# A dense transformer block on one core: the first four products of the MLP placed ahead of the last transposes of the second chunk

## The chip, the cores and the metric

The kernel runs on one core of a Trainium2 chip. The metric is the device time of one execution in microseconds (us), as the median of several runs.

## The reference

One block works on 2048 tokens of width 1024 in fp32. An input projection feeds attention and a pooling mixer; both are merged by gates, go through an output projection, and then

```python
x = _layernorm(ALPHA * x + g1 * y, ln1_g[l], ln1_b[l])
x = _mlp_sublayer(x, sh2, sc2, g2, w_mlp_in[l], w_mlp_out[l], ln2_g[l], ln2_b[l])

def _mlp_sublayer(z, shift, scale, gate, w1, w2, g, b):
    u = _modulate(z, shift, scale)            # _layernorm(z) * (1 + scale) + shift
    h = jnp.square(jax.nn.relu(u @ w1)) @ w2  # w1 1024 x 4096, w2 4096 x 1024
    return _layernorm(ALPHA * z + gate * h, g, b)
```

The change lies where the normalised tokens become the operand of `u @ w1`.

## The kernel before

**Stages.** Attention comes first, over all tokens. Then the merge, the output projection and the first normalisation run over two chunks of 1024 tokens, `c` = 0 and 1. Then comes the MLP's first product for both chunks, and then its second.

**The end of a chunk.** `out_mm` accumulates the output projection of one block of 128 tokens (`b`, 8 in a chunk); `ln_affine` normalises it, SP stores it as x1 (L956), and `ln1_u` normalises it again into a tile `xn` (`normal`, L900 on ACT). `u2_half(h)` turns four such blocks into the MLP's operand: for each of four pairs of 128 columns (`kp`), PE transposes eight 128x128 tiles (L929), ACT scales and shifts the two results into `u2f` (L930), and POOL forms four sums and differences `u2s` of quarters (L935 to L938). SP stores the three quarters that go as they are (L941) and the four combinations (L942). These are the seven *planes* of the scratch `us_scr[c]`. Half 0 runs inside the block loop; half 1 is put into the list `late`. Chunk 0's is run within chunk 1; chunk 1's is run behind the loop by `run(late)`, ahead of the MLP.

**The MLP's first product** multiplies 2x2 block matrices with seven products in place of eight. `us_scr[c]` holds the seven left operands, one plane each. The right operands are made from the weights of one `Pair` (256 columns of w1): `Pair.load` brings them into `sraw` (L1001, two DMAs of half a megabyte), `Pair.add` makes their combinations on POOL (`ext`, L1009 to L1011). fp32 is computed as three products of two rounded parts: `split` casts to the high part on ACT (L59) and subtracts it on DVE for the low part (L62). `Pair.step` splits a right operand into a tile `R` (8 buffers); `l_fill` loads a plane into `rw` (L1085, one DMA of a megabyte, 2 buffers) and splits it in two halves into `La` or `Lb`; all seven planes of a chunk stay for its 16 pairs. `Pair.prod` is one product: 12 matmuls of 128x512 (4 slices times 3 terms, L1039), and behind it a copy, a sum or a square in tiles `st`.

```python
ORDER = (1, 6, 2, 7, 5, 4, 3)
PLANE = {1: 0, 2: 1, 4: 2, 5: 3, 6: 4, 7: 5, 3: 6}
groups = [pairs[0:2]] + [[q] for q in pairs[2:14]] + [pairs[14:16], pairs[16:18]] + [[q] for q in pairs[18:]]
seq = [(g, p, q) for g in groups for p in ORDER for q in g]
```

So pairs 0 and 1 go together: the first four products of `seq` are product 1 of both and product 6 of both, 48 matmuls on planes 1 and 6; product 2 is next. Right operands are prepared `AHEAD` = 7 products ahead.

**What sets the order.** Each engine works through its own instructions in order, and so does SP, whose queue issues all DMAs here. PE's order is the order in which the code is written (`manual_schedule`); the other engines' is set by a scheduler when the kernel is built. Memory comes from pools that open and close like a stack on one side of SBUF: `lpx`, `ptx` and `rpx` hold the tiles of the chunk (with the `xn`, `u2f` and `u2s` slots) and close before `mlp` (`R`, `La`) and `mlp1` (`sraw`, `rw`, `Lb`, `st`, `ext`) open.

Of the kernel before, what the change touches and what calls it, by code (L numbers as in the profile page):

```python
# [16 lines left out]
P = 128  # L17
# [19 lines left out]
def block_kernel(  # L37
# [687 lines left out]
    for c in range(2):  # L725
# [195 lines left out]
        def u2_half(h, c=c, t0=t0, xn=xn, ys=ys):  # L921

            for kp in range(4):
# [38 lines left out]
        late = [lambda f=u2_half: f(1)]  # L962

    sp.dma_start(g2_scr, gb[1][0:1, :].rearrange("a d -> (a d)"))
    run(late)
    lpx.close()
# [11 lines left out]
    mp = ctx.enter_context(sbuf("mlp"))  # L978
    m1 = ExitStack()
    m1p = m1.enter_context(sbuf("mlp1"))  # L980
# [3 lines left out]
    def rtile():  # L984
        return mp.tile([P, 2, 4, P], F32R, name="R", tag="R", bufs=8)

    def sttile(name):
        return m1p.tile([P, 512], F32, name=name, tag="st", bufs=14)
# [3 lines left out]
    class Pair:  # L992
# [5 lines left out]
        def load(self):  # L998
            self.raw = m1p.tile([P, 2, 4, 256], F32, name="sraw", tag="sraw", bufs=3)
            for k in range(2):  # L1000
                sp.dma_start(self.raw[:, k], w1v[:, k, :, self.n * 256:(self.n + 1) * 256])  # L1001
            b11, b12, b21, b22 = self.b = [self.raw[:, k, :, h * P:(h + 1) * P] for k in range(2) for h in range(2)]
            self.op = {1: b11, 2: b21, 3: b22, 4: b11, 7: b12}

        def add(self):
            b11, b12, b21, b22 = self.b
            for p in (5, 6):
                self.op[p] = m1p.tile([P, 4, P], F32, name="ext", tag="ext", bufs=4)
            pool.tensor_tensor(self.op[5], b12, b11, ALU.subtract)  # L1009
            pool.tensor_tensor(self.op[6], b22, self.op[5], ALU.subtract)  # L1010
            pool.tensor_tensor(b12, b22, b12, ALU.subtract)  # L1011
# [70 lines left out]
    def l_fill(c, p):  # L1082

        raw = m1p.tile([P, 4, 512], F32, name="rw", tag="rw", bufs=2)
        sp.dma_start(raw, us_scr[c][:, PLANE[p]])  # L1085
        Lc[c][p] = []
        for j in range(2):
            if (p, j) in ((1, 0), (1, 1), (6, 0)):
                t = m1p.tile([P, 2, 2, 512], F32R, name="Lb", tag="Lb", bufs=3)
            else:  # L1090
                t = mp.tile([P, 2, 2, 512], F32R, name="La", tag="La", bufs=11)
            split(t[:, 0], t[:, 1], raw[:, 2 * j:2 * j + 2])
# [8 lines left out]
    AHEAD = 7  # L1101
    for i in range(AHEAD):
        if i % 2 == 0:
            l_fill(0, ORDER[i // 2])
        prep[i][1].step(prep[i][0])
    for p in ORDER[4:]:
        l_fill(0, p)
    for i, (g, p, q) in enumerate(seq):
        n = q.c * 16 + q.n
        if p == 1 and n + 2 < len(pairs):  # L1110
# [18 lines left out]
    def w2_fill(p, j):  # L1129
# [24 lines left out]
        l = mp.tile([P, 2, 2, 512], F32R, name="La", tag="La", bufs=11)  # L1154
# [3 lines left out]
    L2 = {p: [] for p in ORDER}  # L1158
    R2 = {}
# [160 lines left out]
```

## Time and profile before

| what | value |
|---|---|
| median of 3 runs | 3034.75 us (3033.85 to 3036.7) |
| profiled execution | 3039.96 us, its span 3038.2 us |
| granted clock of TensorE, mean over the span | 0.979 |
| PE busy | 2909.0 us, 96% of the span |
| DVE, ACT, POOL busy | 1819.1, 1369.1, 1380.6 us |
| matmuls of the first MLP product on `La`, on `Lb` | 485.2 us (2112), 139.5 us (576) |
| idle of PE just before the 576 on `Lb` | 25.4 us |

The profiled execution is one of its own, 5.2 us above the median of the others; all moments below are on its clock, in us from the start of the span. The last row of the table is almost all of the idle time that lies between the output projection of the second chunk and the MLP, where the change is made.

### The profile page before, as it was taken

How to read it: one execution, taken by the hardware profiler on the slowest of the kernel's cores; microseconds unless marked ns; L12 is line 12 of the kernel's file. 1: busy time of each engine (PE TensorE's matmuls, PEld its weight loads, DVE VectorE, ACT ScalarE, POOL GpSimd, SP SyncE). 2: the span in 40 equal slices, each digit the busy share in tenths (PEclk: the TensorE clock that was granted, in tenths of full speed). 3: DMA queues.
4: the chain of work that ended last, by engine and by line, in shares of the span. 5: the costliest groups of instructions: out<-in, count | busy, mean ns of one | idle time of the engine just before them, and what ended most of it. 6: DMA issues, size and time to landing. Idle time of an engine off the chain costs nothing. (4 is left out here: it accounts for less than half of the span.)

```text
span 3038.2 us, 42601 instructions
## 1 busy us (share of the span) xinstructions
PE 2909.0 (96%) x15336; PEld 2481.3 (82%) x15336; DVE 1819.1 (60%) x3201; ACT 1369.1 (45%) x2462; POOL 1380.6 (45%) x1638
## 2 busy tenths in 40 slices
PE   8899999999899999899999779999999799999998
PEld 5789989998888888888889668888888587888886
DVE  5577877877875444742144775557555453556675
ACT  3477767777741131432121455556555332333342
POOL 1867777777540014423032556657665240123244
PEclk9999999999999999999999889999999899999999
DMA  7111111112234433342122475547554684566563
GB/s 255 35 32 37 32 37 31 38 42 61 67 100 144 127 125 111 112 144 78 56 97 84 141 263 161 153 149 222 156 153 124 246 308 153 187 215 218 196 209 108
DMA packets 343015, 395.38 MB, mean 130 GB/s; under 512 B 16785, under 2 KB 277009, under 8 KB 341010
## 3 DMA queue, kind: packets, MB, share of 16 engines
q1 hardware_dynamic: 342802, 392.64, 40.5%
q8 instruction: 121, 1.98, 0.3%
q14 instruction: 92, 0.75, 0.1%
HBM read 275.13 MB, written 117.44 MB: 129 GB/s over the span
## 5 line engine op out<-in xcount | busy, mean ns | idle before, releaser
L1220 PE MATMUL ps_y<-La,R 128*128 128x512 f32 x2688 | 619.4, 393 | 25.8 <-ACT R L59 12.1
L1220 PEld LDWEIGHTS ps_y<-La,R 128*128 128x128 f32 x2688 | 508.9, 190 | 136.4 <-ACT La L59 13.7
L1039 PE MATMUL ps_h<-La,R 128*128 128x512 f32 x2112 | 485.2, 390 | 0.3 <-ACT cx L1044 0.3
L1039 PEld LDWEIGHTS ps_h<-La,R 128*128 128x128 f32 x2112 | 397.2, 188 | 83.3 <-ACT cx L1044 0.7
L62 DVE TENSOR_TENSOR R<-hraw,R 128x512 fp32r<-128x512 f32 x224 | 198.0, 890 | 150.7 <-ACT R L59 150.2
L59 ACT CAST R<-hraw 128x512 fp32r<-128x512 f32 x224 | 137.6, 621 | 281.3 <-PE ps_y L1220 272.9
L62 DVE TENSOR_TENSOR pl<-ps_pt,ph 128x512 fp32r<-128x512 f32 x312 | 212.5, 686 | 70.5 <-ACT ph L59 68.6
L465 POOL TENSOR_SCALAR s<-s,sm 128x640 f32<-128x640 f32 (+1 forms) x256 | 201.6, 795 | 103.0 <-DVE sm L464 53.9
L462 ACT ACTIVATE s<-s,sm 128x641 f32<-128x641 f32 (+1 forms) x256 | 209.8, 820 | 70.2 <-DVE sm L456 69.8
L456 DVE CUSTOM_DVE_ANT_0 s<-ps_s,mask,nsink 128x640 f32<-128x640 f32 (+1 forms) x256 | 211.5, 863 | 29.8 <-PE ps_s L451 29.7
L59 ACT CAST ph<-ps_pt 128x512 fp32r<-128x512 f32 x312 | 179.3, 580 | 109.3 <-PE ps_pt L486 106.0
L861 POOL TENSOR_TENSOR sa<-sa,m 128x512 f32<-128x512 f32 x32 | 57.1, 1805 | 374.5 <-DVE sa L860 374.5
L486 PE MATMUL ps_pt<-ident,s 128*128 128x128 f32 x1248 | 189.7, 274 | 12.4 <-DVE pl L62 8.2
L62 DVE TENSOR_TENSOR R<-sraw,R 128x512 fp32r<-128x512 f32 x160 | 146.3, 917 | 77.3 <-ACT R L59 76.8
L59 ACT CAST wh<-raw 128x2048 fp32r<-128x2048 f32 (+1 forms) x38 | 67.0, 1771 | 276.1 <-DMA raw<-w_in 73.6
L486 PEld LDWEIGHTS ps_pt<-ident,s 128*128 128x128 f32 x1248 | 151.6, 141 | 43.1 <-DVE pl L62 11.3
L62 DVE TENSOR_TENSOR wl<-raw,wh 128x2048 fp32r<-128x2048 f32 (+1 forms) x38 | 86.3, 2274 | 159.5 <-ACT wh L59 159.5
L59 ACT CAST R<-sraw 128x512 fp32r<-128x512 f32 x160 | 98.9, 621 | 155.2 <-PE ps_h L1039 97.5
L1039 PE MATMUL ps_h<-Lb,R 128*128 128x512 f32 x576 | 139.5, 396 | 25.4 <-ACT Lb L59 21.9
L1039 PEld LDWEIGHTS ps_h<-Lb,R 128*128 128x128 f32 x576 | 109.8, 191 | 49.7 <-ACT Lb L59 22.3
L66 PE MATMUL ps_out<-wh,mg 128*128 128x256 f32 x512 | 143.1, 281 | 0.0
L67 PE MATMUL ps_out<-wl,mg 128*128 128x256 f32 x512 | 142.8, 280 | 0.0
(264 smaller groups left out, 7098.4 us busy)
## 6 DMA issues: line engine op xcount, KB each, us to landing
hraw<-hs_scr SPq DMA_DIRECT2D x112, 512.0 KB, 4.0
w<-w_mlp_out SPq DMA_DIRECT2D x72, 512.0 KB, 5.4
sraw<-w_mlp_in SPq DMA_DIRECT2D x64, 512.0 KB, 6.3
hs_scr<-s SPq DMA_DIRECT2D x96, 256.0 KB, 4.6
raw<-w_in SPq DMA_DIRECT2D x19, 1024.0 KB, 5.5
raw<-w_ada SPq DMA_DIRECT2D x16, 1024.0 KB, 5.3
rw<-us_scr SPq DMA_DIRECT2D x14, 1024.0 KB, 5.4
raw<-u_scr SPq DMA_DIRECT2D x8, 1032.0 KB, 5.5
```

The costliest lines, as they stand in the source:

```text
L59: act.copy(hi, src)
L62: (lo_eng or dve).tensor_tensor(lo, src, hi.bitcast(F32), ALU.subtract)
L66: pe.matmul(ps, sh, mh, start=first, stop=False)
L67: pe.matmul(ps, sh, ml, start=False, stop=False)
L456: dve.tensor_tensor_reduce(out=s[:, 0:n], in0=pieces[z][2], in1=mk[z], op0=ALU.add, op1=ALU.min, scale=-1.0 / math.sqrt(HD), scalar=nsink[ ...
L462: act.activation(s[:, 0:n + 1], s[:, 0:n + 1], AF.Exp, bias=sm[:, 0, j:j + 1], scale=-1.0, accum_out=sm[:, 1, j:j + 1])
L465: pool.tensor_scalar(s[:, 0:n], s[:, 0:n], sm[:, 2, j:j + 1], 1.0, ALU.mult, ALU.mult)
L486: pe.transpose(pt[:, c:c + P], self.s.probs[2 * z + j][:, o:o + P], ident)
L861: pool.tensor_tensor(s, s, m0[j][:, a:a + m], ALU.add)
L1039: pe.matmul(ps, a, b, start=p in (1, 6, 5) and k == 0 and i == 0, stop=k == 3 and i == 2, skip_group_check=p not in (1, 6, 5))
L1220: pe.matmul(ps, a, b, start=n == 0 and z == 0, stop=n == 15 and z == 2)
```

## The change

`rpx` is still closed behind the chunk loop, but `lpx` stays open on the left side. Two pools, `mlpr` and `mlpr1`, are opened on the right side instead. They hold what the first four products need: all 8 buffers of `R`, four tiles `Le` for the halves of planes 1 and 6, 4 of the 14 `st` buffers (`se`), 2 of the 3 `sraw` buffers. Planes 1 and 6 are loaded as four half planes (L1099, half a megabyte each) into slots of `xs`, in place of two whole ones, and the first two pairs' `ext` lies in `xs` slots too. Chunk 1's half 1 of `u2_half` is cut in four pieces, one for each `kp`, whose `u2f` and `u2s` go to slots of `xs`. After product 4 of `seq` (`EARLY` = 4) these pieces run; then `lpx` is closed, `mlp` and `mlp1` are opened with the remaining buffers (`La` 7, `Lb` 3, `st` 10, `sraw` 1, `rw` 2, `ext` 4), planes 2, 7, 5, 4, 3 are filled (L1094) and pairs 2 and 3 are loaded. In the MLP's second product the left tiles are spread over the two sides in the same way (4 `Le` and 7 `La` for 11). Each engine executes as many instructions as before, SP two DMAs more.

```diff
--- before.py
+++ after.py
@@ -918,9 +918,9 @@
             normal(n, accs[b])
             xn.append(n)
 
-        def u2_half(h, c=c, t0=t0, xn=xn, ys=ys):
-
-            for kp in range(4):
+        def u2_half(h, kps=range(4), c=c, t0=t0, xn=xn, ys=ys):
+
+            for kp in kps:
                 f = slot(ys, 0, [P, 2, 512], F32, "u2f")
                 for kk in range(2):
                     k = 2 * kp + kk
@@ -959,11 +959,9 @@
             if b == 5:
                 u2_half(0)
         ln1_u(7)
-        late = [lambda f=u2_half: f(1)]
+        late = [lambda f=u2_half: f(1)] if c == 0 else [lambda kp=kp, f=u2_half, s=xs: f(1, (kp,), ys=s) for kp in range(4)]
 
     sp.dma_start(g2_scr, gb[1][0:1, :].rearrange("a d -> (a d)"))
-    run(late)
-    lpx.close()
     ptx.close()
     rpx.close()
 
@@ -975,17 +973,23 @@
 
     ORDER = (1, 6, 2, 7, 5, 4, 3)
     PLANE = {1: 0, 2: 1, 4: 2, 5: 3, 6: 4, 7: 5, 3: 6}
-    mp = ctx.enter_context(sbuf("mlp"))
+    ep = ctx.enter_context(sbuf("mlpr", side="right"))
     m1 = ExitStack()
-    m1p = m1.enter_context(sbuf("mlp1"))
+    e1 = m1.enter_context(sbuf("mlpr1", side="right"))
     ms3 = ExitStack()
     ms3.enter_context(tc.manual_schedule(engines={mybir.EngineType.PE}))
 
     def rtile():
-        return mp.tile([P, 2, 4, P], F32R, name="R", tag="R", bufs=8)
+        return ep.tile([P, 2, 4, P], F32R, name="R", tag="R", bufs=8)
+
+    m1p = None
+    sts = [0]
 
     def sttile(name):
-        return m1p.tile([P, 512], F32, name=name, tag="st", bufs=14)
+
+        n = sts[0] = (sts[0] + 1) % 14
+        pl, tag, bufs = (e1, "se", 4) if 1 <= n <= 4 else (m1p, "st", 10)
+        return pl.tile([P, 512], F32, name=name, tag=tag, bufs=bufs)
 
     w1v = w_mlp_in.rearrange("(k two p) n -> p two k n", two=2, p=P)
 
@@ -996,7 +1000,8 @@
             self.c, self.n, self.R = c, n, {}
 
         def load(self):
-            self.raw = m1p.tile([P, 2, 4, 256], F32, name="sraw", tag="sraw", bufs=3)
+            pl, bufs = (e1, 2) if (16 * self.c + self.n) % 3 < 2 else (m1p, 1)
+            self.raw = pl.tile([P, 2, 4, 256], F32, name="sraw", tag="sraw", bufs=bufs)
             for k in range(2):
                 sp.dma_start(self.raw[:, k], w1v[:, k, :, self.n * 256:(self.n + 1) * 256])
             b11, b12, b21, b22 = self.b = [self.raw[:, k, :, h * P:(h + 1) * P] for k in range(2) for h in range(2)]
@@ -1004,7 +1009,10 @@
 
         def add(self):
             b11, b12, b21, b22 = self.b
-            for p in (5, 6):
+            if m1p is None:
+                t = slot(xs, 1, [P, 2, 4, P], F32, "ext")
+                self.op.update({5: t[:, 0], 6: t[:, 1]})
+            for p in (5, 6) if m1p else ():
                 self.op[p] = m1p.tile([P, 4, P], F32, name="ext", tag="ext", bufs=4)
             pool.tensor_tensor(self.op[5], b12, b11, ALU.subtract)
             pool.tensor_tensor(self.op[6], b22, self.op[5], ALU.subtract)
@@ -1081,15 +1089,23 @@
 
     def l_fill(c, p):
 
-        raw = m1p.tile([P, 4, 512], F32, name="rw", tag="rw", bufs=2)
-        sp.dma_start(raw, us_scr[c][:, PLANE[p]])
+        if m1p is not None:
+            raw = m1p.tile([P, 4, 512], F32, name="rw", tag="rw", bufs=2)
+            sp.dma_start(raw, us_scr[c][:, PLANE[p]])
         Lc[c][p] = []
         for j in range(2):
-            if (p, j) in ((1, 0), (1, 1), (6, 0)):
+            if m1p is None:
+                half = slot(xs, 0, [P, 2, 512], F32, "rw")
+                sp.dma_start(half, us_scr[c][:, PLANE[p], 2 * j:2 * j + 2])
+            else:
+                half = raw[:, 2 * j:2 * j + 2]
+            if p in (1, 6):
+                t = ep.tile([P, 2, 2, 512], F32R, name="Le", tag="Le", bufs=4)
+            elif (p, j) in ((4, 1), (3, 0), (3, 1)):
                 t = m1p.tile([P, 2, 2, 512], F32R, name="Lb", tag="Lb", bufs=3)
             else:
-                t = mp.tile([P, 2, 2, 512], F32R, name="La", tag="La", bufs=11)
-            split(t[:, 0], t[:, 1], raw[:, 2 * j:2 * j + 2])
+                t = mp.tile([P, 2, 2, 512], F32R, name="La", tag="La", bufs=7)
+            split(t[:, 0], t[:, 1], half)
             Lc[c][p].append(t)
 
     pairs = [Pair(c, n) for c in range(2) for n in range(16)]
@@ -1099,15 +1115,23 @@
         q.load()
     prep = [(p, q) for _, p, q in seq]
     AHEAD = 7
+    EARLY = 4
     for i in range(AHEAD):
-        if i % 2 == 0:
+        if i in (0, 2):
             l_fill(0, ORDER[i // 2])
         prep[i][1].step(prep[i][0])
-    for p in ORDER[4:]:
-        l_fill(0, p)
     for i, (g, p, q) in enumerate(seq):
         n = q.c * 16 + q.n
-        if p == 1 and n + 2 < len(pairs):
+        if i == EARLY:
+            run(late)
+            lpx.close()
+            mp = ctx.enter_context(sbuf("mlp"))
+            m1p = m1.enter_context(sbuf("mlp1"))
+            for z in ORDER[2:]:
+                l_fill(0, z)
+            for z in (2, 3):
+                pairs[z].load()
+        if i >= EARLY and n + 2 >= 4 and p == 1 and n + 2 < len(pairs):
             pairs[n + 2].load()
         q.prod(p, Lc[q.c][p])
         if q is pairs[15]:
@@ -1151,11 +1175,14 @@
             pool.tensor_tensor(t, t, t2, ALU.subtract)
         else:
             t = b(1, 1)
-        l = mp.tile([P, 2, 2, 512], F32R, name="La", tag="La", bufs=11)
+        n = lns[0] = (lns[0] + 1) % 11
+        pl, tag, bufs = (ep, "Le", 4) if 1 <= n <= 4 else (mp, "La", 7)
+        l = pl.tile([P, 2, 2, 512], F32R, name="La", tag=tag, bufs=bufs)
         split(l[:, 0], l[:, 1], t)
         L2[p].append(l)
 
     L2 = {p: [] for p in ORDER}
+    lns = [0]
     R2 = {}
 
     def h_fill(p, i):
```

PE, from the transposes of half 1 of chunk 1 to the first products. Before (`ps_u` are the transposes, `ps_h` the products; a row is one run of equal instructions):

```order
L929 MATMUL ps_u_18090<-ident,xn 128x128 x4
L929 MATMUL ps_u_18106<-ident,xn 128x128 x4
L929 MATMUL ps_u_18112<-ident,xn 128x128 x4
L1039 MATMUL ps_h_18236<-Lb,R 128x512 x12
L1039 MATMUL ps_h_18257<-Lb,R 128x512 x12
L1039 MATMUL ps_h_18275<-Lb,R 128x512 x6
```

The same place after, from the third of the four products on:

```order
L1047 MATMUL ps_h_18142<-Le,R 128x512 x12
L1047 MATMUL ps_h_18160<-Le,R 128x512 x12
L929 MATMUL ps_u_18179<-ident,xn 128x128 x4
L929 MATMUL ps_u_18185<-ident,xn 128x128 x4
L929 MATMUL ps_u_18201<-ident,xn 128x128 x4
L929 MATMUL ps_u_18207<-ident,xn 128x128 x4
L929 MATMUL ps_u_18223<-ident,xn 128x128 x4
L929 MATMUL ps_u_18229<-ident,xn 128x128 x4
L929 MATMUL ps_u_18245<-ident,xn 128x128 x4
L929 MATMUL ps_u_18251<-ident,xn 128x128 x4
L1047 MATMUL ps_h_18106<-La,R 128x512 x12
```

The 48 matmuls of the first four products now stand ahead of the transposes of half 1, and product 2, on `La`, directly behind the last of these.

SP, the last stores of chunk 1 (`us_scr_62`) and the first loads of the MLP (weights, and planes from chunk 0's `us_scr_61`). Before:

```order
L942 DMA us_scr_62<-u2s 128x4x256
L941 DMA us_scr_62<-u2f 128x2x128 x6
L942 DMA us_scr_62<-u2s 128x4x256
L941 DMA us_scr_62<-u2f 128x2x128 x6
L942 DMA us_scr_62<-u2s 128x4x256 x3
L1001 DMA sraw<-w_mlp_in 128x4x256 x4
L1085 DMA rw<-us_scr_61 128x2048 x2
L1001 DMA sraw<-w_mlp_in 128x4x256 x2
L1085 DMA rw<-us_scr_61 128x2048 x5
```

The same place after:

```order
L942 DMA us_scr_62<-u2s 128x4x256
L1006 DMA sraw<-w_mlp_in 128x4x256 x4
L941 DMA us_scr_62<-u2f 128x2x128 x9
L942 DMA us_scr_62<-u2s 128x4x256
L941 DMA us_scr_62<-u2f 128x2x128 x3
L942 DMA us_scr_62<-u2s 128x4x256 x3
L1094 DMA rw<-us_scr_61 128x2048 x2
L1006 DMA sraw<-w_mlp_in 128x4x256 x2
L1094 DMA rw<-us_scr_61 128x2048 x2
```

The weights of the first two pairs now go ahead of the stores of half 1, planes 2 and 7 directly behind them.

SP earlier, among the stores of x1 of chunk 1 (`x_scr`), as a piece of the difference:

```order
 L667 DMA raw<-w_out 128x8x256
-L956 DMA x_scr<-acc 128x1024 x5
+L956 DMA x_scr<-acc 128x1024 x2
+L1099 DMA rw<-us_scr_61 128x1024 x2
+L956 DMA x_scr<-acc 128x1024
+L1099 DMA rw<-us_scr_61 128x1024
+L956 DMA x_scr<-acc 128x1024
+L1099 DMA rw<-us_scr_61 128x1024
+L956 DMA x_scr<-acc 128x1024
 L941 DMA us_scr_62<-u2f 128x2x128 x3
```

The four half planes of the first four products are loaded there.

## Rows read from the trace of the kernel before

**Rows 1.** The page's first part: busy us, share of the span, instructions.

```profile
PE 2909.0 (96%) x15336; PEld 2481.3 (82%) x15336; DVE 1819.1 (60%) x3201; ACT 1369.1 (45%) x2462; POOL 1380.6 (45%) x1638
```

**Rows 2.** PE's timeline: start, length, line, operation, count, idle before and releaser.

```profile
1711.25 1.04 PE L929 MATMUL ps_u<-ident,xn 128*128 128x128 f32 x8
...
1734.94 5.94 PE L929 MATMUL ps_u<-ident,xn 128*128 128x128 f32 x24 [0.66 <-ACT u2f L930]
1762.78 0.79 PE L1039 MATMUL ps_h<-Lb,R 128*128 128x512 f32 x1 [21.89 <-ACT Lb L59]
1764.07 7.77 PE L1039 MATMUL ps_h<-Lb,R 128*128 128x512 f32 x24 [0.50 <-DVE Lb L62]
1774.81 2.09 PE L1039 MATMUL ps_h<-Lb,R 128*128 128x512 f32 x5 [2.97 <-DVE Lb L62]
...
1780.41 28.73 PE L1039 MATMUL ps_h<-La,R 128*128 128x512 f32 x126
```

**Rows 3.** Windows: length, busy PE, PEld, DVE, ACT, POOL, clock, DMA share, GB/s.

```profile
1767.00:1768.00 1.00, 1.00 (x4) 0.79 (x3) 1.00 (x2) 1.00 (x2) 1.00 (x2) 0.50 0.91 139
...
1769.00:1770.00 1.00, 1.00 (x6) 0.84 (x5) 1.00 (x2) 1.00 (x2) 0.92 (x2) 1.00 0.97 410
...
1774.00:1775.00 1.00, 0.19 (x1) 0.20 (x2) 1.00 (x2) 0.42 (x1) 0.00 (x0) 1.00 0.00 0
...
1776.00:1777.00 1.00, 1.00 (x4) 0.81 (x3) 1.00 (x2) 0.00 (x0) 0.00 (x0) 0.50 0.40 66
...
1779.00:1780.00 1.00, 1.00 (x6) 0.80 (x5) 1.00 (x3) 0.62 (x1) 0.00 (x0) 1.00 0.97 410
```

**Rows 4.** ACT's timeline: the last normalisation, the first scalings, the first casts.

```profile
1732.31 1.24 ACT L900 ACTIVATE xn<-acc,nm,mv 128x1024 f32<-128x1024 f32 x1 [0.92 <-DVE nm L899]
...
1734.11 1.45 ACT L930 ACTIVATE u2f<-ps_u,mod 128x512 f32<-128x512 f32 x2 [0.57 <-PE ps_u L929]
...
1761.68 1.99 ACT L59 CAST Lb<-rw 128x1024 fp32r<-128x1024 f32 x2 [3.64 <-DMA rw<-us_scr]
```

**Rows 5.** DVE's timeline: subtractions of the split.

```profile
1754.57 1.34 DVE L62 TENSOR_TENSOR R<-sraw,R 128x512 fp32r<-128x512 f32 x1 [22.36 <-ACT R L59]
...
1762.75 3.49 DVE L62 TENSOR_TENSOR Lb<-rw,Lb 128x1024 fp32r<-128x1024 f32 x2 [2.28 <-ACT Lb L59]
...
1774.67 1.21 DVE L62 TENSOR_TENSOR La<-rw,La 128x1024 fp32r<-128x1024 f32 x1
```

**Rows 6.** POOL's timeline: combinations of half 1 (first, last), then of the weights.

```profile
1734.97 0.73 POOL L937 TENSOR_TENSOR u2s<-u2f 128x256 f32<-128x256 f32 x1 [4.43 <-ACT u2f L930]
...
1744.66 1.40 POOL L938 TENSOR_TENSOR u2s<-u2f,u2s 128x256 f32<-128x256 f32 x2
1754.10 1.26 POOL L1009 TENSOR_TENSOR ext<-sraw 128x512 f32<-128x512 f32 x1 [8.04 <-issue]
...
1761.67 1.26 POOL L1010 TENSOR_TENSOR ext<-sraw,ext 128x512 f32<-128x512 f32 x1
```

**Rows 7.** SP's timeline: issues of stores and of the first weights.

```profile
1730.56 0.36 SPq L942 DMA_DIRECT2D us_scr<-u2s  x1
...
1744.00 2.45 SPq L942 DMA_DIRECT2D us_scr<-u2s  x3
1746.54 3.88 SPq L1001 DMA_DIRECT2D sraw<-w_mlp_in  x4
```

**Rows 8.** The first weight load, issued at 1746.54: time to landing.

```profile
DMA to landing us min/median/max: 7.4/7.4/7.4
```

**Rows 9.** Nine plane loads issued from 1740 to 1800: time to landing.

```profile
DMA to landing us min/median/max: 4.8/6.9/12.5
```

**Rows 10.** The two plane loads behind the weights: issue, time to landing.

```profile
L1085 SPq DMA_DIRECT2D rw<-us_scr x2: 823/972/1122, 1750.5 to 1751.6; - x2
...
DMA to landing us min/median/max: 11.0/11.8/12.5
```

**Rows 11.** Two plane loads issued at 1795.6 and 1797.0: time to landing.

```profile
DMA to landing us min/median/max: 8.5/9.1/9.7
```

## The prediction

> **What bounds the kernel now.** I read the page's first part, then PE's rows of the stretch in which the MLP begins, then the clock of the same stretch, and last the rows of ACT, DVE, POOL and the DMA queue there. TensorE is busy for 96% of the span [rows 1], so elsewhere a change can only win where PE stands still, and the change touches one such place. PE ends the second chunk's output projection at 1711.3 and has only transposes until 1740.9; then it waits 21.9 us, until 1762.78, for the first split tile of the MLP. After 24 matmuls it waits again, 3.0 us, and from 1774.8 on it runs without a pause [rows 2]. The products of planes 2, 7, 5, 4, 3 of the first two pairs are 120 of the 126 matmuls of the run that starts at 1780.41; at 28.73 / 126 = 0.228 us each they begin at 1780.41 + 28.73 - 120 x 0.228 = **1781.8**. All work before and behind that point is the same in both kernels, so what the change is worth is how much earlier these 120 can begin, less any pauses among them.
>
> Why PE waits: ACT normalises the last token block until 1733.55, scales the transposes from 1734.11 on [rows 4], POOL makes 16 combinations out of them until 1746.06 [rows 6], SP stores three of their results from 1744.00 and only then, at 1746.54, issues the first weight load [rows 7]. The first weights land 7.4 us after their issue [rows 8], the plane behind them after 11.0 us [rows 10]; cast and split follow.
>
> **The change, step by step.** All times are of the profiled execution.
>
> (A) The first product. SP now issues the weights behind the store of 1730.56 [rows 7], at about 1731.0 instead of 1746.54. With the 7.4 us of [rows 8] they land at 1738.4, or sooner, since less is queued ahead. The four half planes are loaded among the stores of the token blocks and lie ready. ACT takes them behind the last normalisation: four casts at 1.99 / 2 us each [rows 4], 1733.55 to 1737.5. DVE subtracts behind it: four at between 1.21 us and 3.49 / 2 = 1.75 us, then the weights' own at 1.34 us [rows 5]. The third matmul needs that last one: 1734.6 + 4 x 1.21 + 1.34 = 1740.8 to 1734.6 + 4 x 1.75 + 1.34 = 1742.9. POOL is idle in the first half of this and at work in the second, so I take 1742.
>
> [...] A subtraction took 1.21 us while POOL did nothing and 1.75 us where it worked [rows 3, 5, 6]. [...] The trace shows 0.54 us for each, and the sum goes by the trace.
>
> (B) The four products. They are 48 matmuls; two run ahead of the third's wait, 46 x 0.228 = 10.5 us. [...] So the products end at 1742 + 10.5 + 2.3 = **1754.8**. Their later weights don't hold them up: POOL's six operations that lead to the second pair's combination took from 1754.10 to 1762.93, 8.8 us [rows 6], now 1738.4 + 8.8 = 1747.2, and cast and subtraction are over by 1750, where the fourth product begins at about 1752.
>
> (C) The last transposes stand behind these four products, and with them ACT's scaling, POOL's combinations and the stores. ACT also holds one weight cast (half as wide as those of [rows 4], so 0.5 us) that waits for the fourth product's end, ahead of the first scaling; 0.75 us with the first transposes. From the first scaling to the last combination it was 1746.06 - 1734.11 = 11.95 us [rows 4, 6], set by 16 POOL operations of 0.69 us in a row. They are not shortened: the last one ends at 1754.8 + 0.75 + 11.95 = **1767.5**, 21.4 us later than before.
>
> (D) Plane 2 is the first work behind, and its load is queued on SP behind the last store: issue 0.5 us after the last combination, 1768.0. Of nine loads of a plane the quickest landed after 4.8 us [rows 9]. The weights behind the same three stores took 7.4 us for half a megabyte [rows 8]; a plane has a whole one, and a megabyte more adds 2.6 us at the margin (the plane loads of 1750.5 and 1751.6 landed after 11.0 and 12.5 us [rows 10], at 1761.5 and 1764.1), so half of one adds 1.3. So 4.8 to 8.7 us. The stores are now a little further apart and no weights are ahead, so I take 6: landed at 1774.0.
>
> (E) Cast 1.0 us and subtraction 1.21 us [rows 4, 5]: first matmul at 1775.0, the rest from 1776.2. PE has paused some 14 us since the last transposes. A pause of 3.0 us, from 1771.8 to 1774.8, was followed by a granted clock of 0.50 at 1776, with 1.00 back at 1779 [rows 2, 3], so I charge a second slow start: 2.3 us, less 0.3 us that pass in the wait for the subtraction. Counted in full-speed matmuls, plane 2 begins at 1776.2 + 2.0 - 0.2 = **1778.0**.
>
> [...]
>
> (F) The planes behind. A plane costs PE 24 x 0.228 = 5.5 us. Plane 7 lands 2.6 us behind plane 2 and is split by 1779, wanted at 1783.5. The two staging buffers come free at about 1777.4 and 1780; planes 5 and 4 land by 1785 and 1788 even behind one megabyte of weights, are split by 1787 and 1790, and are wanted at 1789 and 1794.4. Plane 3 goes behind another megabyte, lands by 1795.5, split by 1797.7, wanted at 1799.9. The cover is 2 us at two of them: close, but held.
>
> What else moves costs nothing that I can find. The four early loads stand on SP among the stores of the token blocks; what they wait for is over by then, and nobody but later stores waits behind them. The new pools keep each ring as long as it was (4 + 10 for 14, 2 + 1 for 3, 4 + 7 for 11), and on every engine the order of the instructions beyond the first two pairs is what it was but for one copy and one cast that trade places with a neighbour, so the rest of the MLP keeps its time.
>
> The sum: 1781.8 - 1778.0 = **3.8 us gained**. The profiled execution has 3039.96 us around a span of 3038.2; its neighbours' median is 3034.75. 3034.75 - 3.8 = 3031.0. A measurement of this kernel tells about 0.2% from no change, which is 6.1 us, so this counts as the same.
>
> **Rivals.**
> 1. *More is won.* The subtractions run at 1.21 us (1.2 us less in A), the wait for the third matmul passes part of the slow start (0.8 us in B), plane 2 lands after 4.8 us (1.2 us), and half of the second slow start passes in waiting (0.8 us): 3.8 + 4.0 = 7.8 us, 3027.0. For it: half of the nine plane loads landed within 6.9 us [rows 9]. Against it: three stores stand right ahead.
> 2. *The gain is eaten by the late chain.* The 16 combinations and the load still follow one another and only start later. The third matmul at 1742.9 (0.9 us more), a second slow start inside the four products, where PE waits between first and third matmul (2.3 us), and plane 2 after 7.4 us (1.4 us): 3.8 - 4.6 = -0.8, 3035.6. In this case the move does not do what it says; it only swaps one wait for another.
> 3. *Slower: the supply of planes becomes the bound.* Each staging buffer is filled, cast and subtracted before its next load goes out, and two of them serve planes 2 to 3 just as PE wants one each 5.5 us; before, the 10 matmul-filled microseconds of products 1 and 6 lay ahead as a cushion. If loads take 12.5 us, as one did behind weights [rows 10], one turn of a buffer is 12.5 + 2.0 + 1.75 = 16.25 us, 8.1 us a plane, and four planes lose 4 x (8.1 - 5.5) = 10.6 us: 6.8 us slower, 3041.6. It decides from (8.1 - 5.5 being 0.95) a turn of 12.9 us, a landing of 9.1 us. For it: 8.5 to 9.7 us at 1795 [rows 11]. Against it: the 12.5 us had two megabytes of weights ahead, and now one lies between.
>
> **How the numbers follow.** My forecast, a gain of 1 to 6 us, 0.48; the first rival 0.28; the second 0.16; the third 0.08. Faster by over 0.2% is the first rival alone, 0.28; within 0.2% are forecast and second rival, 0.64; slower is the third, 0.08. The range goes from the first rival's time to the second's, each with a margin of 1.4 us, half of what the three runs of the kernel before lie apart (3033.85 to 3036.7): 3025.6 to 3037.0. Left out are the third rival and the far end of the first, some 0.18 together.
>
> **What would show it.** In the changed kernel: the first product's matmuls at about 1738 to 1742 and the fourth's end at 1753 to 1757; POOL's last combination at 1766 to 1769; plane 2's load issued half a microsecond later and landed 5 to 8 us after that; a granted clock of 0.50 again when product 2 begins, at about 1775; and no pause of PE from there to the third pair. The prediction fails if the four products take longer than 15 us, if the combinations don't follow at 0.69 us each, or if PE waits for planes 5 to 3.

## The result and the profile after

The changed kernel takes 3070.07 us (median of 4 runs, 3069.78 to 3071.9) beside 3035.2 us (4 runs, 3033.85 to 3036.7) for the kernel before: a ratio of 1.0115, with a 95% interval of 1.01 to 1.013. It is 35 us slower. The forecast was 3031.0 us, with a range of 3025.6 to 3037.0, and no rival reached that far.

The page's first part of the changed kernel, and its costliest groups (line, output and operands, count | busy us, mean ns | idle ahead). The last row is the kernel before, for the first of the groups:

```profile
PE 2936.3 (96%) x15336; PEld 2480.8 (81%) x15336; DVE 1798.8 (59%) x3201; ACT 1367.8 (45%) x2462; POOL 1381.3 (45%) x1638
...
L1247 PE MATMUL ps_y<-La,R 128*128 128x512 f32 x2688 | 633.6, 398 | 23.4 <-ACT R L59 11.9
...
L1047 PE MATMUL ps_h<-La,R 128*128 128x512 f32 x1344 | 324.5, 400 | 24.0 <-ACT La L59 16.1
```

```profile
L1220 PE MATMUL ps_y<-La,R 128*128 128x512 f32 x2688 | 619.4, 393 | 25.8 <-ACT R L59 12.1
```

As many instructions as before, but PE is busy 27.3 us longer [rows 1], so most of the loss is no wait: the same matmuls take longer. (The mean is the length of one matmul, 398 ns in the first group; neighbours overlap, so the step from one to the next is read off the starts of rows.) The two groups are all of the MLP's second product and half of its first. PE's timeline of the changed kernel says where (start, length, line, operation, count, idle before and releaser):

```profile
1708.36 1.04 PE L929 MATMUL ps_u<-ident,xn 128*128 128x128 f32 x8
...
1737.96 12.52 PE L1047 MATMUL ps_h<-Le,R 128*128 128x512 f32 x46 [0.18 <-DVE R L62]
...
1772.44 0.79 PE L1047 MATMUL ps_h<-La,R 128*128 128x512 f32 x1 [16.14 <-ACT La L59]
...
1804.10 5.63 PE L1047 MATMUL ps_h<-Le,R 128*128 128x512 f32 x24
1816.36 11.83 PE L1047 MATMUL ps_h<-La,R 128*128 128x512 f32 x42 [6.62 <-ACT cx L1052]
...
1832.23 5.64 PE L1047 MATMUL ps_h<-Le,R 128*128 128x512 f32 x24
1837.71 9.98 PE L1047 MATMUL ps_h<-La,R 128*128 128x512 f32 x42
1847.52 4.36 PE L1047 MATMUL ps_h<-Lb,R 128*128 128x512 f32 x18
1851.72 5.64 PE L1047 MATMUL ps_h<-Le,R 128*128 128x512 f32 x24
```

The kernel before, in the third pair, the fourth, the start of the fifth, and where the second product of the MLP begins:

```profile
1808.99 4.24 PE L1039 MATMUL ps_h<-Lb,R 128*128 128x512 f32 x18
...
1828.03 4.24 PE L1039 MATMUL ps_h<-Lb,R 128*128 128x512 f32 x18
...
1847.07 4.24 PE L1039 MATMUL ps_h<-Lb,R 128*128 128x512 f32 x18
...
2393.03 3.76 PE L1220 MATMUL ps_y<-La,R 128*128 128x512 f32 x7 [12.12 <-ACT R L59]
```

A pair began with `Lb` and now begins with `Le`, so the same points can be laid beside each other:

| point | before | after | difference |
|---|---|---|---|
| last full row of half 0's transposes, ahead of the change | 1711.25 | 1708.36 | -2.9 |
| third pair begins | 1808.99 | 1804.10 | -4.9 |
| fourth pair begins | 1828.03 | 1832.23 | +4.2 |
| fifth pair begins | 1847.07 | 1851.72 | +4.65 |
| MLP's second product begins | 2393.03 | 2410.53 | +17.5 |
| span ends | 3038.2 | 3067.7 | +29.5 |

The first line is difference between executions. Up to the third pair the change has gained 2.0 us. In the third pair 9.1 us are lost. From then on each pair loses 0.45 us or so (19.49 for 19.04), 13 us in 29 of them, and the MLP's second product loses 12. (The profiled execution of before lay 5 us above its median, so the medians differ by more than the spans.) There are two faults, and neither stands in the stretch that was rewritten.

**Slower matmuls.** Windows of 100 us without a pause, before and after (busy PE with its count, PEld, DVE, ACT, POOL, clock, DMA share, GB/s):

```profile
1900.00:2000.00 100.00, 100.00 (x443) 82.81 (x442) 51.47 (x64) 51.57 (x86) 58.68 (x41) 1.00 0.51 149
```

```profile
1900.00:2000.00 100.00, 100.00 (x433) 80.89 (x432) 49.59 (x62) 49.62 (x83) 58.73 (x41) 1.00 0.50 146
```

PE is never idle and the granted clock is 1.00 in both, yet 10 matmuls fewer pass. By the starts of the rows above, 42 on `La` take 47.52 - 37.71 = 9.81 us, 233.6 ns each, and 24 on `Le` 5.48 us, 228 ns; before, every pair of 84 took 19.04 us, 226.7 ns each. So in the changed kernel a matmul takes 233.6 or 228 ns by the operand it reads. `R` and `Le` now lie on the right side of SBUF, `La` and `Lb` on the left.

**A wait for a store.** ACT's copy that frees the accumulators in the third pair, and SP's queue ahead of it, in the changed kernel:

```profile
1815.72 0.59 ACT L1052 COPY cx<-ps_h 128x512 f32<-128x512 f32 x1 [7.63 <-DMA hs_scr<-cx]
```

```profile
1807.19 1.18 SPq L1006 DMA_DIRECT2D sraw<-w_mlp_in  x2
1808.46 0.53 SPq L1035 DMA_DIRECT2D hs_scr<-cx  x1
```

The copy wants an `st` buffer whose old content is still on its way to memory: the store was issued at 1808.46 behind two weight loads and took 7.2 us to land. PE stands 6.62 us and then starts at a granted clock of 0.50 (window from 1817 to 1818, below), with 42 matmuls in 11.83 us for 9.98.

### The profile page after: what moved, and what is told of

The parts are those of the page before. It is cut to its first block, busy times and chain, and to the rows that moved or that the text cites. A ratio compares the mean times of both kernels' runs of the same rounds, so it can differ in the third digit from the quotient of the medians.

```text
span 3067.7 us, 42601 instructions
## 1 busy us (share of the span) xinstructions
PE 2936.3 (96%) x15336; PEld 2480.8 (81%) x15336; DVE 1798.8 (59%) x3201; ACT 1367.8 (45%) x2462; POOL 1381.3 (45%) x1638
## 4 chain that ended last, share of the span: by engine, by line
PE 83%; DVE 5%; DMA 5%; POOL 3%; issue 2%; ACT 1%; SPq 0%; POOLq 0%; DVEq 0%; ACTq 0%
PE ps_y L1247 18%; PE ps_h L1047 18%; PE ps_o L503 4%; PE ps_pt L486 4%; PE ps_s L450 3%; PE ps_gp L688 2%; PE ps_ga L685 2%; PE ps_ga L688 2%; PE ps_ga L686 2%; PE ps_ab L685 2%; PE ps_ab L686 2%; PE ps_gp L685 2%; PE ps_ab L688 2%; PE ps_gp L686 2%; PE ps_s L451 2%
## 5 line engine op out<-in xcount | busy, mean ns | idle before, releaser
L1247 PE MATMUL ps_y<-La,R 128*128 128x512 f32 x2688 | 633.6, 398 | 23.4 <-ACT R L59 11.9
L1047 PE MATMUL ps_h<-La,R 128*128 128x512 f32 x1344 | 324.5, 400 | 24.0 <-ACT La L59 16.1
L1047 PEld LDWEIGHTS ps_h<-La,R 128*128 128x128 f32 x1344 | 255.5, 190 | 87.5 <-ACT La L59 16.4
L1047 PE MATMUL ps_h<-Le,R 128*128 128x512 f32 x768 | 182.5, 394 | 19.5 <-ACT R L59 19.3
L1047 PEld LDWEIGHTS ps_h<-Le,R 128*128 128x128 f32 x768 | 145.5, 190 | 52.4 <-ACT R L59 19.7
L62 DVE TENSOR_TENSOR R<-sraw,R 128x512 fp32r<-128x512 f32 x160 | 139.1, 872 | 65.2 <-ACT R L59 64.7
```

The source lines that it names most:

```text
L62: (lo_eng or dve).tensor_tensor(lo, src, hi.bitcast(F32), ALU.subtract)
L1047: pe.matmul(ps, a, b, start=p in (1, 6, 5) and k == 0 and i == 0, stop=k == 3 and i == 2, skip_group_check=p not in (1, 6, 5))
L1247: pe.matmul(ps, a, b, start=n == 0 and z == 0, stop=n == 15 and z == 2)
```

## Experiments

Theory 1: the cadence of matmuls depends on the distance in bytes, along a partition, between the weights' address and the moving operand's, modulo some power of two. In the program before, `R` starts at 2624 and `La`, `Lb` at 35392 and 166464: differences of whole multiples of 256. In the changed one `R` starts at 196576, `La` at 2624, `Lb` at 76352, `Le` at 163808: weights less operand, that is 160 modulo 256 for the slow two (96 the other way round, a series of e1) and 0 for `Le`. All addresses are those of the built program. Rival: the sides themselves are at fault (weights far from the operand), or other engines' traffic. Theory 2: the ring of 14 `st` buffers, cut into 4 and 10 by a fixed count, gives the third pair's copy one of four buffers that all hold long-lived tiles, where one ring gave it the first that came free. Rival: the store is late by itself, whatever the ring.

**Distances alone (e1).** A kernel that leaves the whole block out and runs series of 96 matmuls on one tile; a name w32m64 has the weights 32 and the moving operand 64 bytes past two addresses that lie a multiple of 256 bytes apart (the tile itself begins at 1216, 192 bytes past such a multiple); `h` and `l` stand for high and low in SBUF.

```diff
+def case(name, w, m, count=96):
+    t = ps.tile([P, 512], F32, name=name, tag="c", bufs=6)
+    for k in range(count):
+        wo, mo = w + 128 * (k % 8), m + 512 * (k % 4)
+        pe.matmul(t, b[:, wo:wo + 128], b[:, mo:mo + 512], start=k == 0, stop=k == count - 1)
```

> This kernel leaves the whole block out: it runs only series of 96 matmuls of 128x512 in fp32r behind 800 others, and writes a corner of the output. In each series the weights and the moving operand lie in one large tile at chosen byte offsets (series w0m32: weights 0, moving operand 32 bytes behind a multiple of 128; lw and hw: weights in the lower or the upper end of the tile, moving operand in the other). The traces so far: 226.7 ns from one matmul to the next in the MLP of the kernel before, 233.3 ns in the changed one wherever the right operand R lay on the right side and the left operand on the left. Theory 1, the offset of one operand against the other: 226.7 ns for w0m0, w0m64, w0m128, w32m32 and 233 ns for w0m32, w32m0, w64m32; the far series do as their offsets say, 226.7 ns with (0, 0) and (32, 32). Theory 2, the place: all series with both operands near each other take 226.7 ns whatever their offset, and the series with weights high and moving operand low take 233 ns whatever their offset.

PE's timeline, one row a series:

```profile
326.86 22.15 PE L66 MATMUL w0m64z<-B 128*128 128x512 f32 x96
348.85 22.56 PE L66 MATMUL w0m96z<-B 128*128 128x512 f32 x96
371.25 22.56 PE L66 MATMUL w0m128z<-B 128*128 128x512 f32 x96
393.65 21.94 PE L66 MATMUL w0m256z<-B 128*128 128x512 f32 x96
415.42 22.57 PE L66 MATMUL w0m288z<-B 128*128 128x512 f32 x96
...
460.22 21.95 PE L66 MATMUL w32m32z<-B 128*128 128x512 f32 x96
482.00 22.35 PE L66 MATMUL w16m16z<-B 128*128 128x512 f32 x96
504.19 22.55 PE L66 MATMUL w16m0z<-B 128*128 128x512 f32 x96
526.58 22.56 PE L66 MATMUL w64m0z<-B 128*128 128x512 f32 x96
...
593.14 21.92 PE L66 MATMUL hw0lm0z<-B 128*128 128x512 f32 x96
```

Starts of neighbouring rows are 96 matmuls apart. At a distance of 128 that is 393.65 - 371.25 = 22.40 us, 233.3 ns each; at 256 it is 415.42 - 393.65 = 21.77 us, 226.7 ns each. By their lengths the series at 0 go with the second, all but one, and those at 288, 96 and 32 with the first. Two things are less simple. With both operands 16 bytes on (w16m16) the distance is 0 too, but a matmul took (504.19 - 482.00) / 96 = 231.1 ns, where w32m32 took 226.9. So the distance alone does not decide; in the MLP, where all tiles begin at a multiple of 32, only the series with such starts apply. And the sign counts: the moving operand 64 bytes on (w0m64) took 229.1 ns, the weights 64 bytes on (w64m0) 233.3. Nothing else runs (DVE, ACT and POOL are busy for 0.00 us in six windows of the series), so other engines' traffic is out; far apart (hw0lm0, 21.92 us) is as fast as near (w0m256, 21.94 us), so the sides are out. The first form of the theory, by which 64 and 128 would be fast, was wrong: in these series 226.7 to 226.9 ns came at multiples of 256 alone.

**A pad of 32 bytes (e2)**, which makes the distance 128:

```diff
+ctx.enter_context(sbuf("padr", side="right")).tile([P, 8], F32, name="pad")
 ep = ctx.enter_context(sbuf("mlpr", side="right"))
```

> The changed kernel with 32 unused bytes at the top of the right side, so that R and Le begin at a multiple of 64 bytes as La and Lb do. Theory 1 (offset of R against La and Lb): every matmul of the MLP back at 226.7 ns, some 13.5 us less in the first product and 12 us in the second, 3070 - 26 = 3044 us. Theory 2 (R on the other side of the memory): 233.3 ns as before, 3070 us. Both: the 6.6 us idle of PE ahead of the third pair's second product stays.

3066.41 us, ratio 1.0102 (1.0087 to 1.0117). Only 3.7 us came back, and no run shows from where; the 42 matmuls of a pair on `La` still take 9.95 us. By e1 a distance of 128 (w0m128, 22.56 us) is as slow as 160 (w0m96, 22.56 us).

**The fault put into the kernel before (e3).** Only 32 bytes go between `R` and the planes; nothing of the change is in it:

```diff
+rpool = ctx.enter_context(sbuf("mlpR"))
+padp = ctx.enter_context(sbuf("mlppad"))
 mp = ctx.enter_context(sbuf("mlp"))
+padp.tile([P, 8], F32, name="pad", tag="pad", bufs=1)
```

> The kernel before with 32 unused bytes between R and the planes, so that La and Lb lie 32 bytes off R's alignment, with everything still on the left side in the old order. Theory 1: all 5376 matmuls of the MLP go from 226.7 to 233.3 ns, 5376 x 6.67 ns = 36 us, 3035 + 36 = 3071 us. Theory 2: no change, 3035 us.

3069.93 us, ratio 1.0117 (1.01 to 1.0134): 32 bytes make it as slow as the whole change did, close to the 3071 us of Theory 1. (That both kernels take the same time is chance: here all 5376 matmuls of the MLP lie 32 bytes off, and PE's rows from 1794.77 to 1862 have no pause.) PE's timeline:

```profile
1825.10 4.36 PE L1042 MATMUL ps_h<-Lb,R 128*128 128x512 f32 x18
...
1844.70 4.36 PE L1042 MATMUL ps_h<-Lb,R 128*128 128x512 f32 x18
```

A pair of 84 takes 19.60 us, 233.3 ns a matmul: here all operands are off, in the changed kernel `Le` was not.

**The ring (e4).** The changed kernel, with the four right buffers given to tiles that come free in time:

```diff
-n = sts[0] = (sts[0] + 1) % 14
-pl, tag, bufs = (e1, "se", 4) if 1 <= n <= 4 else (m1p, "st", 10)
+n = sts[0]
+sts[0] += 1
+early = n < 4 if n < 14 else n % 14 in (4, 5, 6, 13)
+pl, tag, bufs = (e1, "se", 4) if early else (m1p, "st", 10)
```

> The changed kernel with another choice of which result tiles lie in the four right-hand buffers: from the third pair on the copy of product 1 (cx) goes to a left-hand buffer, whichever is free first, and the four right-hand buffers take s1, s2, s4 of one pair and s4 of the next. Theory A (the split of the ring makes the third pair's cx wait for the first pair's cx to be stored): the 6.6 us idle of PE and the slow clock behind it (42 matmuls in 11.83 us instead of 9.98) go, 8.5 us less, 3061.5 us. Theory B (cx is late because the store itself is late, behind the weights on SP's queue, and any buffer would be as late): 3068 to 3070 us. The matmuls stay at 233.3 ns in both.

3059.28 us, ratio 1.0079 (1.0064 to 1.0094), 10.8 us less than the changed kernel. ACT's copy and PE's row behind the third pair's first 24:

```profile
1808.30 0.57 ACT L1054 COPY cx<-ps_h 128x512 f32<-128x512 f32 x1
```

```profile
1804.48 5.64 PE L1049 MATMUL ps_h<-Le,R 128*128 128x512 f32 x24
1809.96 9.98 PE L1049 MATMUL ps_h<-La,R 128*128 128x512 f32 x42
```

The copy comes 7.4 us earlier and PE does not pause. The gain is larger than the 8.5 us of Theory A; the changed kernel has a later wait for such a copy too, 0.80 us at 2100.28. The store's own delay is not the cause; the fixed choice of buffers is.

**The pad of 160 bytes (e5), and with the ring (e6).** e5 is e2 with `[P, 40]` in place of `[P, 8]`, a distance of 0; e6 adds e4's edit.

> The changed kernel with 160 unused bytes at the top of the right side, so that the distance from R and Le to La and Lb is a multiple of 256 bytes, as all of R, La, Lb were to one another in the kernel before. In the run of the offsets the distances 0 and 256 took 226.7 ns, 32, 96 and 128 took 233.3 ns. Theory 1 in the form that this gives (the distance modulo 256 counts): all matmuls of the MLP at 226.7 ns, 3070 - 26 = 3044 us. Rival (something else on the right side slows them): 3066 us as with 32 bytes.

3044.0 us, ratio 1.0025 (1.0015 to 1.0034): 26.1 us back. In PE's timeline the wait for the copy is still there, and the 42 behind it are at full cadence:

```profile
1816.15 11.27 PE L1048 MATMUL ps_h<-La,R 128*128 128x512 f32 x42 [7.61 <-ACT cx L1053]
...
1836.77 9.68 PE L1048 MATMUL ps_h<-La,R 128*128 128x512 f32 x42
```

> Both repairs together: 160 unused bytes and the other choice of result tiles. What is then left of the change is the move that the prediction costed. If both losses add up, 3044 - 10.8 = 3033 us, 2 us faster than before; as forecast (a gain of 3.8 us) 3031 us; if the move itself is worth nothing, 3035 us.

3032.78 us, ratio 0.9989 (0.998 to 0.9998), 3.5 us less than the kernel before in the same series (3036.24). The two repairs add up: 3070.07 - 26.1 - 10.8 = 3033.2. This is the change without its two faults, and it is what the forecast spoke of. Its PE timeline, the first row for the shift between executions:

```profile
1709.44 1.04 PE L929 MATMUL ps_u<-ident,xn 128*128 128x128 f32 x8
...
1773.44 0.80 PE L1050 MATMUL ps_h<-La,R 128*128 128x512 f32 x1 [15.94 <-ACT La L59]
...
1799.88 4.15 PE L1050 MATMUL ps_h<-Lb,R 128*128 128x512 f32 x17 [0.49 <-DVE Lb L62]
1803.86 5.60 PE L1050 MATMUL ps_h<-Le,R 128*128 128x512 f32 x24
```

The third pair begins 5.1 us earlier than before, of which 1.8 us lay ahead of the stretch: 3.3 us gained.

**What the order itself is worth (e7).** e6 with the transposes put back ahead of the four products; only the early loads and the split memory remain of the change.

```diff
+run(late)
+late = []
 for i, (g, p, q) in enumerate(seq):
```

> As the run with both repairs, but the transposes of half 1 stand ahead of the four products again, in PE's order and for the scheduler; the early loads, the right side and the plane loads behind the last stores stay. Theory P (the gain comes from the four products being ahead of the transposes): it goes, 3035 us or more. Theory S (what counts is when POOL has made the last of the 16 combinations, since plane 2 is loaded behind their stores): 8 weight combinations at about 1.5 us and 16 others at 0.7 us end at about 1736 + 23 = 1759 instead of 1764, product 2 begins 5 us earlier, 3028 us.

3033.04 us, ratio 0.9988 (0.9979 to 0.9997): the same as e6, and neither the time of Theory P nor that of Theory S. The chain of combinations starts earlier but runs slower: six in a row, begun from 1747.05 to 1752.78, take 1.18 to 1.21 us each (in e6 most take 0.72 us, as [rows 6] have it, 0.73), and weight combinations of POOL stand in between. ACT's casts of weights, each with its subtraction on DVE behind it, begin from 1745.87 to 1752.25 beside them. POOL's first, then SP:

```profile
1749.34 1.19 POOL L937 TENSOR_TENSOR u2s<-u2f 128x256 f32<-128x256 f32 x1
```

```profile
1762.17 2.50 SPq L1097 DMA_DIRECT2D rw<-us_scr  x2
```

Plane 2 is issued at 1762.17 and lands 8.1 us later; PE starts on it at 1771.43, after 16.50 us of waiting (15.94 in e6). From half 0's last full row of transposes to the start of the third pair it is 95.2 us, in e6 94.4, before 97.7. So nearly all of the 3.5 us comes from what e7 keeps, the early loads and the memory for them, and at most some 1 us from the products standing ahead of the transposes.

**A shorter chain of combinations (e8).** e6 with two of the four late combinations of each piece on DVE:

```diff
-pool.tensor_tensor(sv[0], a21, a22, ALU.add)
+e = dve if len(kps) == 1 else pool
+e.tensor_tensor(sv[0], a21, a22, ALU.add)
 ...
-pool.tensor_tensor(sv[2], a11, a21, ALU.subtract)
+e.tensor_tensor(sv[2], a11, a21, ALU.subtract)
```

> As the run with both repairs, and two of the four combinations of each piece of half 1 are made on DVE, which is idle then, so that POOL makes 8 behind the four products and not 16. Theory S (the 16 combinations in a row on POOL set when plane 2 is loaded): the last one ends some 5 us earlier, at about 1759, and so does everything behind: 3033 - 5 = 3028 us. Rival (the load of plane 2 behind the weights and stores on the queue sets it): no more than 1 us.

3032.45 us, ratio 0.9985 (0.9976 to 0.9994): no gain over e6. POOL's last combination, then SP:

```profile
1759.88 0.72 POOL L939 TENSOR_TENSOR u2s<-u2f,u2s 128x256 f32<-128x256 f32 x1
```

```profile
1762.69 0.44 SPq L943 DMA_DIRECT2D us_scr<-u2s  x1
1763.18 1.77 SPq L1098 DMA_DIRECT2D rw<-us_scr  x2
```

POOL ends at 1760.6, but SP issues 16 stores from 1751.46 to 1763.13, and plane 2 stands behind them. Counted from half 0's last full row, POOL ends 2.4 us earlier than in e6, but plane 2 is issued only 0.4 us earlier. The queue took the place of the chain.

**The queue (e9).** e6 with planes 2 and 7 issued by ACT, and `rw` in memory that is free earlier:

```diff
-raw = m1p.tile([P, 4, 512], F32, name="rw", tag="rw", bufs=2)
-sp.dma_start(raw, us_scr[c][:, PLANE[p]])
+raw = mp.tile([P, 4, 512], F32, name="rw", tag="rw", bufs=2)
+(act if c == 0 and p in (2, 7) else sp).dma_start(raw, us_scr[c][:, PLANE[p]])
```

> As the run with both repairs, in the changed kernel's order, but the two staging buffers of the planes lie where the output projection's weights lay (free since then), and planes 2 and 7 are issued from ACT's queue, behind its last scaling, instead of SP's behind the last store. Theory Q (the place behind the stores on SP's queue holds product 2 back): the loads go out at about 1759.5 and 1762 instead of 1765.6 and 1766.5, product 2 begins some 5 us earlier and 3033 - 4 = 3029 us are left, since planes 5 and 4 stay where they are. Rival (the stores' own traffic holds the load back, on whatever queue): no change, 3033 us.

3032.17 us, ratio 0.9982 (0.9973 to 0.9991). The kernel before took 3037.83 us in this series, so that the gain is 5.7 us beside e6's 3.5, some 2 us where Theory Q had 4, and the intervals of the two overlap. Plane 2 went out at 1759.83 (plane 7 only at 1766.6) and PE's wait fell from 15.94 to 10.09 us, but waits of 1.30, 0.57, 0.32 and 0.76 us for the planes behind it came instead: this is the third rival of the prediction, in small.

**Both (e10), and DVE's share on top (e11).** Transposes first as in e7, and planes 2 and 7 on ACT's queue ahead of the casts:

```diff
+l_fill(0, 1)
+l_fill(0, 6)
+run(late)
+lpx.close()
 ...
+for z in (2, 7):
+    raws[z] = mp.tile([P, 4, 512], F32, name="rw", tag="rw", bufs=2)
+    act.dma_start(raws[z], us_scr[0][:, PLANE[z]])
 for i in range(AHEAD):
     prep[i][1].step(prep[i][0])
```

> The same, with the transposes of half 1 ahead of the four products as in the run late_first; planes 2 and 7 are issued from ACT's queue behind the copies of product 1, at about 1750. Theory Q: product 2 follows the four products with a pause of a few us instead of 16; the next wait is for planes 5 and 4, which SP loads behind the stores of half 1 at about 1762, landed at 1769, so that some 8 to 12 us are won: 3021 to 3025 us. If the combinations on POOL are the bound in every order: 3030 us or more.

3027.14 us, ratio 0.997 (0.9958 to 0.9981) beside 3037.83 for the kernel before in that series: 0.3% faster than the kernel before, and some 7 us better than e6 where 8 to 12 were expected. The other queue and the other memory of `rw` were not tried apart. PE's timeline:

```profile
1755.65 5.75 PE L1050 MATMUL ps_h<-Le,R 128*128 128x512 f32 x12 [3.21 <-ACT R L59]
...
1768.42 5.83 PE L1050 MATMUL ps_h<-La,R 128*128 128x512 f32 x25
```

The long pause ahead of product 2 is gone; what is left are waits for the split weights of product 6, 3.21 us and two shorter ones.

> The same again, with two of four combinations of each piece of half 1 on DVE. The stores of half 1 end earlier on SP, and with them the loads of planes 5 and 4: another 2 to 4 us less than the run before, 3018 to 3022 us. If DVE's own splits are delayed by as much: the same as the run before.

3027.95 us, ratio 0.9969 (0.9958 to 0.998), the same as e10. POOL's last combination of half 1 ends at 1747.2 instead of 1751.3, but the weights' combinations behind it hardly start earlier (1752.34 in e10, there after 1.02 us):

```profile
1751.70 1.26 POOL L1021 TENSOR_TENSOR ext<-sraw 128x512 f32<-128x512 f32 x1 [4.48 <-DMA us_scr<-u2f]
```

By the profile they wait for a store of half 1, and product 6, where PE waits, needs them. So the next bound seems to be these stores and the memory that they free, not planes 5 and 4 as was expected; no run tests it.

## Why the prediction was wrong

**The moved stretch went as forecast.** The moments of the changed kernel, beside the forecast less the 2.9 us by which this execution ran early:

| step | forecast, shifted | measured |
|---|---|---|
| A, third matmul | 1739.1 | 1737.96 |
| B, four products end | 1751.9 | 1750.5 |
| C, last combination ends | 1764.6 | 1764.09 |
| D, plane 2 issued, landed after | 1765.1, 6 us | 1764.57, 6.7 us |
| E, first matmul on plane 2 | 1772.1 | 1772.44 |

Of C and D the rows in the changed kernel are POOL's last combinations and SP's issue behind them:

```profile
1762.69 1.40 POOL L938 TENSOR_TENSOR u2s<-u2f,u2s 128x256 f32<-128x256 f32 x2
```

```profile
1764.57 2.13 SPq L1094 DMA_DIRECT2D rw<-us_scr  x2
```

Both slow starts came where they were charged, and one more: windows of the changed kernel in the first four products, in product 2, and behind the wait for the store, each at a granted clock of 0.50.

```profile
1740.00:1741.00 1.00, 1.00 (x4) 0.81 (x3) 1.00 (x2) 0.04 (x1) 1.00 (x2) 0.50 0.00 0
...
1775.00:1776.00 1.00, 1.00 (x4) 0.71 (x4) 1.00 (x1) 0.84 (x1) 0.00 (x0) 0.50 1.06 355
1817.00:1818.00 1.00, 1.00 (x4) 0.81 (x3) 0.96 (x2) 0.00 (x0) 0.92 (x2) 0.50 1.14 340
```

The 2.3 us that B and E count for each of the two rest on [rows 2] and [rows 3]: the 24 matmuls from 1764.07 took 7.77 us where 24 x 0.228 is 5.5, with the clock at 0.50 at 1767 and 1.00 at 1769. In the changed kernel the 46 matmuls of B took 12.52 us where 46 x 0.228 is 10.5, 2.0 us more.

Sizes were off by a little: the chain from first scaling to last combination took 13.0 us (1751.09 to 1764.09), not 11.95, and the products ended 1.4 us earlier; in C the two nearly cancel, which is luck. Step F held in the changed kernel; in e6 plane 3 was late by 0.49 us. The forecast gain of 3.8 us stands beside 3.3 in e6's trace and 3.5 in its median. The sum was right for this order; that the order earns the gain it did not show, and by e7 nearly all of it comes without.

DVE and POOL beside each other cost nothing beyond the sum in step A: DVE's four subtractions of planes ran from 1731.60 to 1736.23 and POOL took up work at 1735.94 only. The fifth, of the weights, lay beside POOL's combination and took 1.36 us, twice the 0.69 of one by itself, but the sum had 1.34 for it. A little later in the changed kernel both engines take longer (DVE's rows, then POOL's):

```profile
1785.67 0.69 DVE L62 TENSOR_TENSOR R<-sraw,R 128x512 fp32r<-128x512 f32 x1
...
1788.01 1.22 DVE L62 TENSOR_TENSOR Lb<-rw,Lb 128x1024 fp32r<-128x1024 f32 x1
1789.15 1.78 DVE L62 TENSOR_TENSOR R<-sraw,R 128x512 fp32r<-128x512 f32 x1
```

```profile
1788.03 2.35 POOL L1017 TENSOR_TENSOR ext<-sraw 128x512 f32<-128x512 f32 x1 [6.98 <-DMA sraw<-w_mlp_in]
```

POOL's combination, 1.26 us by itself [rows 6], took 2.35 beside a subtraction of 1.22, and the next subtraction, 0.69 by itself, took 1.78 and ended 0.55 us behind the combination: 1.09 us more for each of the two. The prediction was wrong to take 0.54 us, a mean over two (one of them took 2.30 us), as the price of each. POOL's first two combinations of half 1 in the changed kernel, from 1751.94, took 1.30 and 1.23 us with subtractions of 0.68 us beside them, the later ones 0.72. What makes the two engines wait, no run shows.

**The step that failed is the paragraph "What else moves costs nothing that I can find".** It looked for costs among instructions, queues and lengths of rings, and had one sentence for the memory: "The new pools keep each ring as long as it was (4 + 10 for 14, 2 + 1 for 3, 4 + 7 for 11) [...] so the rest of the MLP keeps its time." The counts are right; what was concluded from them is false.

- *A ring in two parts is not the ring.* With one ring of 14 the third pair of the kernel before took its 19.04 us without a pause; 4 + 10 by count gives each tile a given part. Four long-lived tiles fell on the four right buffers, and the next one had to wait for a store, ACT for 7.63 us. This cost 10.8 us (e4), or 11.2 (e5 against e6).
- *The addresses moved.* `R` came to lie 160 bytes, modulo 256, from the planes on the left. Of the first product's 2688 matmuls the 1344 on `La` and 576 on `Lb`, and 1680 of the second's 2688 (those whose left tile lies on the left), then run at 233.3 ns instead of 226.7: (1920 + 1680) x 6.6 ns = 24 us, beside 26.1 measured (e5). The other 1776 lie at distance 0, but the 24 on `Le` between slow ones took 228.3 ns each; at 1.6 ns more, an estimate from that row, they add 2.8 us.

Together with the gain that gives 26 + 11 - 3 = 34 us, beside 34.9 between the medians. No rival held either mechanism. The third, on supply, did not occur in the changed kernel, and the chance of 0.08 for slower rested on it alone. The trace of before showed 0.228 us a matmul, and I took it as a constant of the shape; that a stage's cadence could depend on where its operands lie was nowhere among the costs that were bounded from both sides.

e1 shows that the pair of addresses matters, by 3% of a matmul (233.3 ns for 226.7); what gets in the way, no run here shows.

What stays open: the mechanism behind the 256 bytes, and whether other stages of this kernel lose by it. The window from 1500 to 1600 of the kernel before holds 434 matmuls at a granted clock of 1.00, where the one from 1900 to 2000 in the MLP holds 443. In the built program the weights `av` of that stage begin at all multiples of 32 modulo 256; moving those operands was not tried.

## What to carry to other kernels

When a change moves a pool, look at the addresses too: compare the addresses of weights and moving operand modulo 256 before and after, and multiply any difference in cadence (here 233.3 ns for 226.7) by all matmuls that use them, far beyond the rewritten lines. A ring that is cut into fixed parts has to be followed tile by tile, by who lives long in which part. And test the order and the layout apart: here the new order was worth next to nothing, the early loads 3.5 us, the early loads with the old order and two plane loads on another queue some 10, and two unseen faults of layout cost 37.

## What was not expected of the hardware

At a granted clock of 1.00, fp32 matmuls in rounded parts of 128x512 ran 226.7 to 226.9 ns apart when the weights' and the moving operand's addresses differed by a multiple of 256 bytes and both began at a multiple of 32; with both 16 bytes past one it was 231.1 ns. They ran some 233.3 ns apart with the moving operand 8, 32, 96, 128 or 288 bytes on, 229.1 ns at 64 (but 233.3 with the weights 64 on), and 236.9 ns at 4 (all e1). 32 bytes in the wrong place cost a kernel of 3035 us some 35 us (e3).
